# Input projection: query latent first, the other 1024 columns as seven Strassen products chained in four PSUM banks, and the local attention by halves of the rows

## The chip, the cores and the metric

One core of a Trainium2 chip. Five engines work side by side, each with an instruction queue of its own: TensorE (PE: matmuls and transposes into PSUM banks), VectorE (DVE), ScalarE (ACT), GpSimd (POOL) and SyncE (SP), which here only starts DMAs. They wait for each other by semaphores. The metric is the device time of one execution in microseconds (us); lower is better.

## The reference

One decoder block on 1024 rows of 1024 columns, all in fp32:

```python
h = rmsnorm(x, mix_norm_g)
proj = h @ w_in
# columns of proj: local q 512 | local k 128 | local v 128 | query latent 384 |
#                  key/value latent 256 | rope key 32 | two gates of 1024
qa, ka, va, q_lat, kv_lat, k_r, g_a, g_b = split(proj)
o_a = sliding_window_attention(rope(qa), rope(ka), va, sinks)      # 8 heads of 64, 2 k/v groups, window 128
cq, ckv = rmsnorm(q_lat), rmsnorm(kv_lat)
o_b = causal_attention(cq @ w_uq, ckv @ w_ukv, rope(k_r))          # 8 heads
y = sigmoid(g_a) * (o_a @ w_o_swa) + sigmoid(g_b) * (o_b @ w_o_mla)
x = x + y @ w_out
h = rmsnorm(x, ffn_norm_g)
x = x + (silu(h @ w_gate) * (h @ w_up)) @ w_down
return rmsnorm(x, final_norm_g)
```

The change touches the first matmul, `h @ w_in`, without the gates, and the local (sliding-window) attention behind it.

## The kernel before

**Exact products.** Every fp32 operand is split in a high and a low half (`split`, L259): ScalarE casts the high half (L260), VectorE takes the low half as a difference (L261). `mm3` (L263) makes each product of three matmuls, high by high, high by low, low by high. The first row block is done in raw fp32 instead (L604), before any half is there.

**Input projection, before.** The rows come as eight blocks of 128. For each block x is loaded twice: as it is (`load_xs`), to take the sum of squares (`square`, ScalarE, L498), and transposed (`load_xt`), as the operand. GpSimd turns the mean into an rsqrt (`rstd_of`, L397 and L400) and scales an identity by it (`dg`, L501); TensorE spreads that over all partitions (`rb`, L505); VectorE multiplies the transposed block by it (`normalize`, L508). Blocks 0 to 4 start unnormalised, and the factor is put in behind the product. The columns come in four groups: `kvq` (512: the second half of q, k, v), `qa` (256: the first half of q), `ql` (416: query latent and rope key) and `kl` (256: key/value latent), each for eight row blocks, each with eight steps of k by three matmuls. Behind them VectorE does the rotations (`rope_of`, L473 to L480) and GpSimd and VectorE the norms of the latents (`latent_end`, L780; `kv_out`, L1127). `h` is stored (`h_out`) and loaded again (`load_set`) to form t1 to t4 (`set_of_h`), the differences of quarters of h which the gates' Strassen products need.

**Gates.** They are done by class `Seven`: each pair of column blocks takes seven products of quarter size instead of eight. `mix` makes the sums of weights on GpSimd, `prep` splits them, `gate_step` runs one product. The first of them writes `fa`.

**Local attention.** Sixteen iterations, two k/v groups by eight row blocks, run between the gate products: per iteration three `gate_step`s, the transposed query (`sw_qT`, whose low halves `qs` VectorE makes at L1044 and L1045), the scores (`sw_scores`), exp, transposed probabilities, and the product with v.

**Order.** In this part of the program each engine's instructions stand in the order in which the code is written (`manual_schedule`, `by_hand`): the order was set by hand, a call after the other. Later stages have theirs from a planner, `Plan`, which takes steps with costs and ranks and writes out an order per engine.

Of the kernel before, what the change touches and what calls it, by code (L numbers as in the profile page):

```python
# [189 lines left out]
def hybrid_block_kernel(  # L190
# [129 lines left out]
    def split_g(hi, lo, raw, k0):  # L320
        for k in range(raw.shape[1]):
            g = gT[:, k0 + k:k0 + k + 1]
            nc.scalar.activation(hi[:, k], raw[:, k], AF.Copy, scale=g)
            nc.vector.scalar_tensor_tensor(lo[:, k], raw[:, k], g, hi[:, k].bitcast(F32), op0=ALU.mult,
                                           op1=ALU.subtract)

    def plain(key, src, shape, wide=False, k0=None):
# [95 lines left out]
    xs = {}  # L423
    xt = {}
    rb = {}

    def load_xt(b, pieces=1):
        xt[b] = U("xt", F32, (P, NK, P))
        n = NK // pieces
        for q in range(pieces):  # L430
            nc.sync.dma_start(xt[b][:, n * q:n * q + n], x_t[b][:, n * q:n * q + n])
            if b == 0 and q == 0:
                st.load_to(1)

    def load_xs(b):
        xs[b] = load_x(b)
# [1973 lines left out]
```

## Time and profile before

| | us |
|---|---|
| median of three runs | 1318.87 (1318.67, 1318.87, 1322.04) |
| span of the profiled execution | 1315.7 |
| its TensorE busy | 1305.2 |
| its VectorE, ScalarE, GpSimd busy | 931.0, 637.7, 568.3 |
| its first gate product starts | 138.25 |

The profiled execution has no time of its own beside its span: the span goes from the first to the last instruction, and the median of the runs lies 3.2 us above it, which is the work around the program. The profile's rows give for a group of instructions the line, the engine, the operation, the tiles with their shapes, the count, the busy time and the mean duration of one in nanoseconds, and then the idle time before them and what ended it. A timeline row gives start and length in us.

### The profile page before, as it was taken

Reading aid. Unit: us, or ns where it says so; the run is one execution under the profiler, and the core shown is the slowest. Engines: PE = TensorE matmul, PEld = TensorE weight load, DVE = VectorE, ACT = ScalarE, POOL = GpSimd, SP = SyncE. Lnnn points to the kernel's source line nnn. Section 1 sums busy time; section 2 is a strip of 40 time slices with the busy share of each in tenths; the row PEclk is TensorE's granted clock in tenths of the full one; section 3 lists DMA queues with packets and bytes.
Section 4 is the critical chain, followed back from the end, with each engine's and each line's share of the span. In section 5 each row is a group of like instructions: output and inputs, shape, how many; then the busy total and the mean of one; then the engine's idle time right before and its main releaser. Section 6 shows DMA issues by size and latency. Waiting matters only on the chain.

```text
span 1315.7 us, 18711 instructions
## 1 busy us (share of the span) xinstructions
PE 1305.2 (99%) x6463; PEld 1101.5 (84%) x6463; DVE 931.0 (71%) x1523; ACT 637.7 (48%) x1286; POOL 568.3 (43%) x552
## 2 busy tenths in 40 slices
PE   9999999999999999999999999999999999999997
PEld 6899888888888888888888888888888888888886
DVE  7868777766788874589889765776666555663964
ACT  7434667565578786644464232232323323634441
POOL 2126656553423266310234478775566621022521
PEclk9999999999999999999999999999999999999999
DMA  9454332336500112895231345753454335995504
GB/s 374 164 187 154 114 115 85 127 111 212 164 14 13 46 60 92 319 264 173 108 101 49 128 148 212 268 183 136 165 184 168 130 123 199 386 385 201 176 13 148
DMA packets 81534, 210.49 MB, mean 160 GB/s; under 512 B 9440, under 2 KB 16608, under 8 KB 80736
## 3 DMA queue, kind: packets, MB, share of 16 engines
q1 hardware_dynamic: 78560, 202.48, 43.6%
q0 software_dynamic: 1440, 4.72, 1.9%
q10 hardware_dynamic: 1440, 2.10, 0.5%
q8 instruction: 51, 0.84, 0.3%
q14 instruction: 43, 0.35, 0.1%
HBM read 143.34 MB, written 61.73 MB: 156 GB/s over the span
## 4 chain that ended last, share of the span: by engine, by line
PE 96%; DVE 1%; ACT 1%; DMA 1%; issue 1%; POOL 0%; SPq 0%; ACTq 0%; DVEq 0%; POOLq 0%
PE fa L269 8%; PE fa L268 8%; PE fa L267 8%; PE fb L269 6%; PE fb L268 6%; PE fb L267 6%; PE fd L268 5%; PE fd L269 5%; PE fd L267 5%; PE pTb L1581 2%; PE xo L269 2%; PE xo L268 2%; PE xo L267 2%; PE ob L1619 1%; PE scb L1536 1%; PE ob L1618 1%
## 5 line engine op out<-in xcount | busy, mean ns | idle before, releaser
L261 DVE TENSOR_TENSOR wl<-wr,wl 128x512 fp32r<-128x512 f32 x147 | 145.7, 1013 | 65.2 <-ACT wl L260 64.8
L261 DVE TENSOR_TENSOR lrv<-lr,lrv 128x1024 fp32r<-128x1024 f32 x77 | 104.9, 1395 | 49.8 <-ACT lrv L260 47.1
L260 ACT CAST lrv<-lr 128x1024 fp32r<-128x1024 f32 x77 | 80.1, 1052 | 95.8 <-PE fd L269 59.8
L268 PE MATMUL fd<-lrv 128*128 128x512 f32 x308 | 119.9, 389 | 0.4 <-DVE lrv L261 0.4
L267 PE MATMUL fd<-lrv 128*128 128x512 f32 x308 | 119.8, 389 | 0.0
L269 PE MATMUL fd<-lrv 128*128 128x512 f32 x308 | 119.8, 389 | 0.0
L260 ACT CAST wl<-wr 128x512 fp32r<-128x512 f32 x147 | 85.2, 621 | 3.6 <-DVE wr L962 1.8
L1565 POOL TENSOR_SCALAR p<-p,denb 128x384 f32<-128x384 f32 (+3 forms) x64 | 47.8, 748 | 89.3 <-DVE denb L1561 78.0
L261 DVE TENSOR_TENSOR wl<-sm,wl 128x512 fp32r<-128x512 f32 x59 | 54.3, 945 | 35.7 <-ACT wl L260 35.5
L275 POOL TENSOR_TENSOR wr<-wr,sm 128x512 f32<-128x512 f32 x20 | 30.1, 1506 | 94.2 <-DVE wl L261 94.2
L268 PEld LDWEIGHTS fd<-lrv 128*128 128x128 f32 x308 | 57.8, 188 | 12.9 <-DVE lrv L261 0.9
L267 PEld LDWEIGHTS fd<-lrv 128*128 128x128 f32 x308 | 57.8, 188 | 12.0
L269 PEld LDWEIGHTS fd<-lrv 128*128 128x128 f32 x308 | 57.8, 188 | 11.9
L397 POOL TENSOR_SCALAR ms<-ss 128x1 f32<-128x1 f32 x32 | 10.3, 323 | 113.1 <-ACT xn L2132 62.9
L2044 ACT ACTIVATE act<-sm 128x512 f32<-128x512 f32 x11 | 7.0, 633 | 104.1 <-DVE sm L272 104.1
L272 DVE TENSOR_TENSOR ptl<-pTb,pth 128x512 fp32r<-128x512 f32 (+2 forms) x96 | 49.5, 548 | 9.2 <-ACT pth L1592 8.8
L275 POOL TENSOR_TENSOR sm<-wr,wr 128x512 f32<-128x512 f32 (+1 forms) x36 | 42.0, 1174 | 31.7 <-PE fb L269 26.0
L1556 ACT ACTIVATE p<-scb,nmb 128x384 f32<-128x384 f32 (+3 forms) x64 | 47.9, 748 | 12.5 <-DVE nmb L1551 8.1
L1551 DVE CUSTOM_DVE_ANT_0 scb<-scb,mask 128x384 f32<-128x384 f32 (+3 forms) x64 | 48.3, 760 | 7.7 <-PE scb L1538 7.1
L1592 ACT CAST pth<-pTb 128x512 fp32r<-128x512 f32 (+2 forms) x96 | 43.1, 484 | 10.3 <-PE pTb L1581 10.0
L267 PE MATMUL fb<-t3h,wl 128*128 128x512 f32 x120 | 47.3, 394 | 0.0
L267 PE MATMUL fb<-t2h,wl 128*128 128x512 f32 x120 | 47.1, 393 | 0.0
(404 smaller groups left out, 4259.8 us busy)
## 6 DMA issues: line engine op xcount, KB each, us to landing
lr<-la_d SPq DMA_DIRECT2D x77, 256.0 KB, 5.4
wr<-in_w_gate_dram SPq DMA_DIRECT2D x22, 512.0 KB, 4.3
wr<-in_w_up_dram SPq DMA_DIRECT2D x22, 512.0 KB, 5.0
la_d<-sd SPq DMA_DIRECT2D x22, 512.0 KB, 5.0
wd<-in_w_down_dram SPq DMA_DIRECT2D x22, 512.0 KB, 7.0
rb_d<-wd SPq DMA_DIRECT2D x22, 512.0 KB, 2.6
lr<-rb_d SPq DMA_DIRECT2D x44, 256.0 KB, 5.4
lr<-in_w_down_dram SPq DMA_DIRECT2D x33, 256.0 KB, 5.4
```

The lines of the kernel that those rows point to most:

```text
L260: nc.scalar.copy(hi, src)
L261: (eng or nc.vector).tensor_tensor(lo, src, hi.bitcast(F32), op=ALU.subtract)
L267: nc.tensor.matmul(ps, ah, bh, start=first and i == 0, stop=False, skip_group_check=go_on)
L268: nc.tensor.matmul(ps, ah, bl, start=False, stop=False, skip_group_check=go_on)
L269: nc.tensor.matmul(ps, al, bh, start=False, stop=last and i == n - 1, skip_group_check=go_on)
L272: eng.tensor_tensor(out, a, b, op=ALU.subtract)
L275: eng.tensor_tensor(out, a, b, op=ALU.add)
L1551: nc.vector.tensor_tensor_reduce(s_, s_, m_, 1.0, -NEG, op0=ALU.add, op1=ALU.min, accum_out=nm)
L1556: nc.scalar.activation(p_, s_, AF.Exp, scale=-1.0, bias=t_.pop(("nm", key)), accum_out=den)
L1565: nc.gpsimd.tensor_scalar(p[:, 0:w], p[:, 0:w], den, 0.0, op0=ALU.mult, op1=ALU.add)
L1581: nc.tensor.transpose(pp[:, k], t_["p", key][:, blk(4 * g + k)], ident)
L1592: nc.scalar.copy(hi, pp)
```

## The change

**Query latent first.** TensorE's first row block, in raw fp32, is now one of `ql`'s; then `ql` for the row blocks in the order 0, 4, 1, 5, 2, 6, 3, 7 (`ROWS`). Blocks 0 and 4 are raw, that is, unnormalised; the others wait for `normalize`. The `square`s, `rb`s and so on are steps of a plan now.

**Seven products for the other 1024 columns.** The columns q, k, v and key/value latent are laid out as a matrix of two column blocks `f` by two halves `kh` of the 1024 k, and each quarter in two pieces `kp` (`load_left`: tiles `ws`). With rows 0 to 3 and rows 4 to 7 as the two row blocks, the product is done in Strassen's way. Scaled by the gain on ScalarE (`scale_left`, L1097), the pieces are summed on VectorE (`left_sum`: s0, s1, d1, d2) and split (tiles `wl`, 128x1024); t1 to t4 are formed at once from the normalised blocks, on GpSimd (`t_step`), and split. Product q, piece kp, for the rows t of a half is `product(q, kp, t)`, six matmuls of 512 columns, called (q,kp,t) here. Their order is q = 1, 2, 6, 7, 4, 5, 3, each with kp = 0, 1 and t = 0 to 3; 6 adds to the PSUM banks of 1, 7 to those of 6, 4 to those of 7, and 3 to those of 5. Tile `st` is the bank. ScalarE copies an intermediate state of a bank where it is an output (E1, W1, W2), VectorE adds to it what lies in the other banks (c11, C22, C12). Then come the rotations, and the norms of the key/value latent (`kv_square`, `rstd_in` on GpSimd as tile `rs_k`, `kv_norm` on VectorE, called k4).

**Order.** All engines' order in this stage comes out of a `Plan` named `beg`: `go(name, eng, cost, emit, after, ...)` adds a step, `rank_by_need` ranks each by when its users need it, and tiles are given out from numbered slots, so that a step can wait for the last reader of a slot.

**Stores.** h is no longer stored and loaded again.

**Local attention.** Its iterations are in the order group 0 rows 0 to 3, group 1 rows 0 to 3, group 0 rows 4 to 7, group 1 rows 4 to 7 (`ITS`). The work of rows 4 to 7 that was done in the projection is done between the iterations: v's halves and k's rotation (`late_row`), k's transposes (`late_k`), q's rotation (`late_q`). The sums over v come in four pieces (`V_AT`).

The core of the diff, with the new steps:

```diff
+    for i, b in enumerate(ROWS):
...
+            ps = tl_["ql", b] = (PX if i < 6 else P1)("ql", (P, 416))
+            mm3(ps, [(hT(k, blk(b)), (tl_["wq", k // 2][0][:, k % 2], tl_["wq", k // 2][1][:, k % 2])) for k in range(NK)])
...
+    def product(q, kp, t):
+        if kp == 0:
+            tl_["ps", q, t] = tl_["ps", {6: 1, 7: 6, 4: 7, 3: 5}[q], t] if q in (6, 7, 4, 3) else (PX if q == 1 else P1)("st")
+        wh, wl_, _ = tl_["left", q, kp]
+        hi, lo = quad[{1: (0, 0), 2: (1, 0), 3: (1, 1)}[q]] if q in (1, 2, 3) else hq[B_OF[q]]
+        mm3(tl_["ps", q, t], [((hi[:, k, blk(t)], lo[:, k, blk(t)]), (wh[:, k % 2], wl_[:, k % 2])) for k in (2 * kp, 2 * kp + 1)],
+            first=kp == 0 and q not in (6, 7, 4, 3), last=kp == 1, go_on=q in (6, 7, 4, 3))
...
+        go("rq", t, eng="D", cost=1450, after=[("M", 4, 1, t)] + [("rq", 0)] * (t == 1), emit=rope_q, use=(("U", ("rp", t)), ("U", ("qq", t))), free=(("rp", t),))
...
+        go("k4", t + 4, eng="D", cost=450, port=True, after=[("k3", t + 4)], emit=lambda t=t: kv_norm(half_of("w2", t)[:, 256:512], t + 4))
...
+    go("gx", eng="P", cost=4000, port=True, after=[("gs", 0), ("gs", 1), ("l", "g", 1), ("h", "g", 1)], emit=lambda: gates.mix(0, nc.gpsimd), use=(("U", "gsum"),))
...
+    def late_q(it):
+        b = ITS[it][1]
+        qn = sw[it]["qn"]
+        rope_nat(halves(qn[:, 0:256], 32), 4, 32, tl_["rope_a"][:, 0, b], tl_["rope_a"][:, 1, b], [halves(qn[:, 0:256], 32)])
```

Three places in the order of the engines. First ScalarE, where the third normalised row block (block 2) gets its high half. Before, casts of a block (`hh<-xt`) stand among squares and copies:

```order
L498 ACTIVATE x_305,ss_459<-x_305 128x1024
L583 COPY qn_452<-qn_452 128x256
L530 CAST khd_155<-kT_436 128x128
L530 CAST khd_156<-kT_436 128x128
L498 ACTIVATE x_307,ss_470<-x_307 128x1024
L260 CAST hh_147<-xt_131 128x4x128
L260 CAST hh_151<-xt_131 128x4x128
L260 CAST hh_149<-xt_303 128x4x128
L260 CAST hh_153<-xt_303 128x4x128
```

After, two scalings of a left factor (L1097) stand ahead of the casts of block 2 (`xt_258`), behind the norms of the latents (L997):

```order
L1006 COPY kr_331<-ql_343 128x32
L1097 ACTIVATE ws_378<-ws_378,gT 128x512 x2
L843 CAST hh_120<-xt_258 128x4x128
L843 CAST hh_124<-xt_258 128x4x128
L843 CAST hh_122<-xt_273 128x4x128
L843 CAST hh_126<-xt_273 128x4x128
L843 CAST wl_435<-ws_378 128x1024
L1097 ACTIVATE ws_385<-ws_385,gT 128x512 x2
L1097 ACTIVATE ws_394<-ws_394,gT 128x512 x2
L843 CAST wl_474<-ws_385 128x1024
L843 CAST wl_480<-ws_394 128x1024
```

The first left factor is scaled ahead of block 2's cast. Second, VectorE at the end of the projection. Before, from the first query's low halves (`qs`) to the first gate products' left factors (L962 scales, L1127 normalises a key/value latent block, L261 takes the low half):

```order
L1044 TENSOR_TENSOR qs_1445<-qT_1442,qs_1445 64x2x128
L1045 TENSOR_TENSOR qs_1445<-qT_1442,qs_1445 64x2x128
L962 TENSOR_SCALAR wr_1398<-wr_1398,gT 128x2x128 x4
L261 TENSOR_TENSOR wl_1522<-wr_1398,wl_1522 128x512
L1127 SCALAR_TENSOR_TENSOR lat_1429<-lat_1429,rstd_1435,lg_991 128x256
L962 TENSOR_SCALAR wr_1400<-wr_1400,gT 128x2x128 x4
L275 TENSOR_TENSOR sm_1564<-wr_1398,wr_1400 128x512
L272 TENSOR_TENSOR sm_1564<-sm_1564,wr_1398 128x512
L272 TENSOR_TENSOR wr_1398<-wr_1398 128x512
L1127 SCALAR_TENSOR_TENSOR lat_1477<-lat_1477,rstd_1483,lg_991 128x256
```

After, the last stretch ahead of product 3's second left low half (`wl_1244`): key/value norms (L1190), a gate's low half (`wl_1214`), the rotations of query blocks 2 and 3 (L454 to L457), `qs`:

```order
L295 TENSOR_TENSOR wl_1214<-sm_1177,wl_1214 128x512
L454 TENSOR_TENSOR rp_1218<-st_642,tab_650 128x256 x2
L456 TENSOR_TENSOR qn_1217<-rp_1218 128x4x32
L457 TENSOR_TENSOR qn_1217<-rp_1218 128x4x32
L454 TENSOR_TENSOR rp_1224<-st_668,tab_650 128x256 x2
L456 TENSOR_TENSOR qn_1223<-rp_1224 128x4x32
L457 TENSOR_TENSOR qn_1223<-rp_1224 128x4x32
L1190 SCALAR_TENSOR_TENSOR lat_1073<-st_642,rs_k,tab_278 128x256
L1190 SCALAR_TENSOR_TENSOR lat_1090<-st_668,rs_k,tab_278 128x256
L745 TENSOR_TENSOR qs_1237<-qT_1234,qs_1237 64x2x128
L746 TENSOR_TENSOR qs_1237<-qT_1234,qs_1237 64x2x128
L295 TENSOR_TENSOR wl_1244<-ws_431,wl_1243 128x1024
```

The rotations and norms, which were spread over the stage, stand in one row ahead of that left factor; on GpSimd the rsqrts for the norms (`rs_k`) stand around the sums of the gate's weights (`sm`, `wr`: `mix`). GpSimd before, at the same place:

```order
L397 TENSOR_SCALAR ms_1433<-ss_1431 128x1
L400 TENSOR_TENSOR rstd_1435<-ms_1433,neg_half 128x1
L397 TENSOR_SCALAR ms_1481<-ss_1479 128x1
L400 TENSOR_TENSOR rstd_1483<-ms_1481,neg_half 128x1
L397 TENSOR_SCALAR ms_1514<-ss_1512 128x1
L400 TENSOR_TENSOR rstd_1516<-ms_1514,neg_half 128x1
L397 TENSOR_SCALAR ms_1556<-ss_1554 128x1
L400 TENSOR_TENSOR rstd_1558<-ms_1556,neg_half 128x1
L397 TENSOR_SCALAR ms_1599<-ss_1597 128x1
L400 TENSOR_TENSOR rstd_1601<-ms_1599,neg_half 128x1
```

and after:

```order
L501 TENSOR_TENSOR rs_q<-rs_q,neg_half 128x1
L295 TENSOR_TENSOR xt_163<-xt_163,xt_174 128x256 x2
L501 TENSOR_TENSOR rs_q<-rs_q,neg_half 128x1
L501 TENSOR_TENSOR rs_k<-rs_k,neg_half 128x1 x5
L298 TENSOR_TENSOR sm_1177<-wr_993,wr_1033 128x512
L295 TENSOR_TENSOR sm_1177<-sm_1177,wr_993 128x512
L295 TENSOR_TENSOR wr_993<-wr_993 128x512
L501 TENSOR_TENSOR rs_k<-rs_k,neg_half 128x1
L295 TENSOR_TENSOR wr_1033<-wr_1033,sm_1177 128x256 x2
L501 TENSOR_TENSOR rs_k<-rs_k,neg_half 128x1 x2
```

The rsqrts of the last key/value blocks have moved behind the sums. Third, TensorE at the end of the stage. Before, the last key/value latent block (`kl`) stands just ahead of the first gate product:

```order
L267 MATMUL kl_1719<-wh_1144,hh_151 128x256
L268 MATMUL kl_1719<-wl_1145,hh_151 128x256
L269 MATMUL kl_1719<-wh_1144,hl_152 128x256
L267 MATMUL kl_1719<-wh_1144,hh_151 128x256
L268 MATMUL kl_1719<-wl_1145,hh_151 128x256
L269 MATMUL kl_1719<-wh_1144,hl_152 128x256
L267 MATMUL fa_1764<-hh_147,wl_1522 128x512
L268 MATMUL fa_1764<-hl_148,wl_1522 128x512
L269 MATMUL fa_1764<-hh_147,wl_1522 128x512
```

After, product 3 does, shown where its second piece begins:

```order
L290 MATMUL st_1106<-wl_1124,hh_126 128x512
L291 MATMUL st_1106<-wl_1125,hh_126 128x512
L292 MATMUL st_1106<-wl_1124,hl_127 128x512
L290 MATMUL st_1106<-wl_1124,hh_126 128x512
L291 MATMUL st_1106<-wl_1125,hh_126 128x512
L292 MATMUL st_1106<-wl_1124,hl_127 128x512
L740 MATMUL qT_1234<-ident,qn_1162 128x128 x2
L290 MATMUL st_1046<-wl_1243,hh_126 128x512
L291 MATMUL st_1046<-wl_1244,hh_126 128x512
L292 MATMUL st_1046<-wl_1243,hl_127 128x512
L290 MATMUL st_1046<-wl_1243,hh_126 128x512
```

The transposed query (`qT`) and product 3's second piece (`wl_1243`, `wl_1244`) follow the last product on its first piece (`wl_1124`); the gate product `fa` comes some 40 matmuls later.

More of the change, by code (lines that the diff above doesn't have):

```diff
@@ L318, in halves_of, with plain @@
         return U("wh", F32R, shape), U("wl", F32R, shape)
[L320 to L327, printed above, removed]
+    def plain(key, src, shape, wide=False):
         def load():
@@ L422, in hybrid_block_kernel @@
     in_order.__enter__()
[L423 to L436, printed above, removed]
+    xs, xt, rb = {}, {}, {}
     dgt = U("dg", F32, (P, 8, P))
@@ L789, in hybrid_block_kernel @@
+    make_identity(nc, ident)
+    for _ in range(11):
+        nc.tensor.matmul(P1("warm"), warm[:, 0:P], warm, start=True, stop=True)
+    del warm
+    tri = U("tri", F32, (P, P))
+    make_lower_triangular(nc, tri)
+    nc.vector.tensor_copy(below, tri)
+    del tri
     B_OF = {1: "b11", 2: "b21", 3: "b22", 4: "t4", 5: "t1", 6: "t2", 7: "t3"}
@@ L948, in hybrid_block_kernel @@
     sw = {}
+    ITS = [(g, b) for b0 in (0, 4) for g in range(NG) for b in range(b0, b0 + 4)]
     oa_t = {}
@@ new lines, in hybrid_block_kernel, with square, spread_row @@
+    for j in range(4):
+        go("wh", j, eng="A", cost=1240, emit=lambda j=j: ql_high(j), after=[("L", "w", j)], use=(("V", ("wq", j)),))
+        go("wl", j, eng="D", cost=1250, emit=lambda j=j: ql_low(j), after=[("wh", j)], port=True)
+        go("wf", j, eng="J", cost=0, after=[("wl", j), ("ql", 0)], emit=lambda j=j: tl_.pop(("wr", j)), free=(("wr", j),))
+    def square(b):
+        t = xs.pop(b)
+        nc.scalar.activation(t, t, AF.Square, accum_out=rn[:, b:b + 1])
+    def spread_row(b):
+        rb[b] = P1("rb", (P, P))
+        nc.tensor.matmul(rb[b], ones, dg[:, b % 7], start=True, stop=True)
@@ new lines, in hybrid_block_kernel, with ql_first, ql_row @@
+    go("df", eng="J", cost=0, after=[("sp", b) for b in ROWS], free=("dg",))
+    def ql_first(j):
+        if j == 0:
+            tl_["ql", 0] = PX("ql", (P, 416))
+        for k in (2 * j, 2 * j + 1):
+            nc.tensor.matmul(tl_["ql", 0], tl_["h0"][:, k], tl_["wr", j][:, k % 2], start=k == 0, stop=k == NK - 1)
+        if j == 3:
+            tl_.pop("h0")
+    def ql_row(i, b):
+        if b == 0:
+            ql_first(3)
+        else:
+            ps = tl_["ql", b] = (PX if i < 6 else P1)("ql", (P, 416))
+            mm3(ps, [(hT(k, blk(b)), (tl_["wq", k // 2][0][:, k % 2], tl_["wq", k // 2][1][:, k % 2])) for k in range(NK)])
+        if i == NB - 1:
+            for j in range(4):
+                tl_.pop(("wq", j))
@@ new lines, in gate_part, with gate_src @@
+    def gate_part(q, i):
+        key = (0, q, "g")
+        if key not in gates.left:
+            gates.left[key] = U("wl", F32R, (P, 2, 4, P))
+        return gates.left[key][:, i]
+    def gate_src(q):
+        return gates.sums[(0, "g")][:, 1] if q == 6 else gates.part(0, "g", *{1: (0, 0), 2: (1, 0)}[q])
+    for kh in range(2):
+        go("gs", kh, eng="A", cost=2050, after=[("L", "g", 0, kh)], emit=lambda kh=kh: gates.scale_part(0, kh))
+    go("gx", eng="P", cost=4000, port=True, after=[("gs", 0), ("gs", 1), ("l", "g", 1), ("h", "g", 1)], emit=lambda: gates.mix(0, nc.gpsimd), use=(("U", "gsum"),))
```

871 lines of the change are left out of this document (467 added, 404 removed).

## The prediction

> **What bounds the kernel now.** I read the page first: busy shares, clock, the chain that ended last.
>
> ```profile
> span 1315.7 us, 18711 instructions
> PE 1305.2 (99%) x6463; PEld 1101.5 (84%) x6463; DVE 931.0 (71%) x1523; ACT 637.7 (48%) x1286; POOL 568.3 (43%) x552
> PEclk9999999999999999999999999999999999999999
> PE 96%; DVE 1%; ACT 1%; DMA 1%; issue 1%; POOL 0%; SPq 0%; ACTq 0%; DVEq 0%; POOLq 0%
> ```
>
> TensorE is busy 99% of the span, at full clock, and is 96% of the chain. So a matmul that is removed is worth its own pitch, but only while the other engines keep ahead; and any new wait of TensorE adds its whole length. The timeline of TensorE gives the pitches (start to start) and the borders of the stage:
>
> ```profile
> 1.30 4.65 PE L592 MATMUL warm<-warm 128*128 128x512 bf16 x11 [1.30 <-DVE warm L589]
> 5.79 7.03 PE L604 MATMUL kvq<-wr,h 128*128 128x512 f32 x16
> 12.25 1.03 PE L552 MATMUL kvq<-wv,hh 128*128 128x512 f32 x2
> 16.33 1.98 PE L558 MATMUL kvq<-wv,hh 128*128 128x512 f32 x8
> 18.14 1.98 PE L552 MATMUL kvq<-wv,hh 128*128 128x512 f32 x8
> 35.48 0.28 PE L267 MATMUL qa<-wv,hh 128*128 128x256 f32 x1
> 35.59 0.28 PE L268 MATMUL qa<-wv,hh 128*128 128x256 f32 x1
> 77.60 0.35 PE L267 MATMUL ql<-wh,hh 128*128 128x416 f32 x1
> 77.79 0.35 PE L268 MATMUL ql<-wl,hh 128*128 128x416 f32 x1
> 138.25 0.40 PE L267 MATMUL fa<-hh,wl 128*128 128x512 f32 x1
> ```
>
> A product of 512 columns takes 0.227 us (eight in 16.33 to 18.14), of 256 columns 0.12, of 416 columns 0.19 (0.189 over a row of 24). The first row's raw fp32 products end at 12.25, and the first gate product `fa` starts at 138.25: all of the input projection lies between. The table of busy times by stretch shows the room beside it:
>
> ```profile
> 20.00:40.00 20.00, 20.00 (x111) 17.28 (x110) 18.08 (x39) 13.18 (x33) 6.25 (x12) 1.00 0.70 279
> 100.00:120.00 20.00, 20.00 (x126) 19.87 (x125) 17.74 (x40) 7.78 (x19) 13.35 (x19) 1.00 0.62 202
> 160.00:200.00 40.00, 40.00 (x201) 33.40 (x200) 29.44 (x59) 26.82 (x80) 25.51 (x32) 1.00 0.36 118
> ```
>
> Columns are TensorE, weight load, VectorE, ScalarE, GpSimd. TensorE has no gap in any of them, yet VectorE is 90% busy: it has about 2 us in 20 to spare.
>
> **The change: TensorE's work.** Before, 12.25 to 138.25 holds 168 products `kvq` of 512 columns, 384 of 256 (`qa`, `kl`) and 192 of 416 (`ql`). After, it holds 7 rows of `ql` (7x24x0.189 = 31.8 us), 336 Strassen products of 512 (x0.227 = 76.3) and 26 transposes and scores of 128 columns (at most the 256-column pitch, 3.1). From the same 12.25 that ends at 12.25 + 111.2 = 123.4, which is 14.8 before 138.25, if nothing waits. The raw row has 416 columns instead of 512 and could end 6.46x96/512 = 1.2 us sooner; row 4 then waits for the low halves of its weights on VectorE, so I count nothing. Of the 14.8, four pairs of `k` transposes (8x0.12 = 1.0) come back inside the local attention: they only moved.
>
> **Wait A, after row 4.** The `rb` (the row norms, spread) of rows 1 and 5 now stand behind row 4's 24 products. Behind them VectorE normalises row 1, then row 5, then ScalarE casts and VectorE takes the low half, before row 1 can run. The groups of instructions by shape, from the first 140 us (count, busy, mean ns):
>
> ```profile
> L508 DVE TENSOR_TENSOR xt<-xt,rb 128x1024 f32<-128x1024 f32 x8 | 9.7, 1215 | 0.1
> L261 DVE TENSOR_TENSOR hl<-xt,hh 128x512 fp32r<-128x512 f32 x24 | 15.5, 686 | 3.6 <-ACT hh L260 3.6
> L260 ACT CAST hh<-xt 128x512 fp32r<-128x512 f32 x24 | 13.6, 616 | 8.7 <-DVE xt L508 7.4 <-DMA xt<-in_x_t_dram 1.2
> L323 ACT ACTIVATE wv<-wr,gT 128x512 fp32r<-128x512 f32 x8 | 5.3, 714 | 1.3 <-DMA wr<-in_w_x_dram 1.3
> ```
>
> 1.215 + 0.616 + 0.686 = 2.5, with the `rb` 2.6. The bounds: 1.8 if the products start on the cast alone, 3.7 if row 5's normalising is in front of the low half for all its length (1.215 more).
>
> **Wait B, after row 5.** ScalarE's queue has `scale_left` of the first left factor (two of the 714 ns rows) ahead of the cast that row 2 needs, and that factor's load comes after eight blocks of x, eight of x transposed, the query-latent weights and a table: 16x0.524 + 1.70 + 0.46 + 0.52 = 11.1 MB.
>
> ```profile
> GB/s 0 35 247 365 393 358 363 332 410 418 418 426 403 402 395 430 406 406 401 426 406 406 401 426 406 406 401 399 395 418 414 410 410 246 37 0 8 0 0 0
> DMA packets 4035, 12.62 MB, mean 316 GB/s; under 512 B 576, under 2 KB 832, under 8 KB 4032
> ```
>
> This is the DMA view of the first 40 us, in slices of 1 us: 12.62 MB are in by 34, at some 410 GB/s, so 11.1 MB are in by 30.0, 30.5 with the last packets. Then 1.43 of scaling, 0.62 cast, 0.69 low: row 2 runs at 33.2. TensorE is free at 12.25 + 2.6 + 3x4.54 + 0.8 (`rb`) = 29.3. The wait is 3.8 (2.2 if the loads land a microsecond earlier and the low half is not awaited; 4.5 if later).
>
> **In the middle** VectorE and GpSimd share the stretch as they do not before: the sums for t1 to t4 go to GpSimd in pieces, while VectorE takes low halves. What that costs is in the timelines (VectorE three rows, GpSimd one):
>
> ```profile
> 93.84 0.68 DVE L261 TENSOR_TENSOR t1l<-hr,t1h 128x512 fp32r<-128x512 f32 x1
> 94.45 1.23 DVE L261 TENSOR_TENSOR t3l<-ht,t3h 128x512 fp32r<-128x512 f32 x1
> 95.60 1.23 DVE L261 TENSOR_TENSOR t2l<-ht,t2h 128x512 fp32r<-128x512 f32 x1
> 94.01 2.27 POOL L272 TENSOR_TENSOR h<-hr,ht 128x256 f32<-128x256 f32 x2 [0.81 <-DVE ht L272]
> ```
>
> The same low half takes 0.68 alone and 1.23 beside GpSimd's subtraction. 16 low halves of t by 0.55 are 8.8 us more of VectorE at worst, over some 70 us in which it has about 7 to spare. On SP's queue the last two loads of left factors now stand behind seven stores of latent rows, each of which waits for its row, so the sums for product 6 begin late. I take 2.0 of wait for both, where the low halves of product 6 are late; ends 0 and 6.
>
> **The tail, at product 3.** Only three products and a transpose (18x0.227 + 0.25 = 4.3 us) lie between product (5,1,3) and (3,1,0), whose left low half VectorE makes. In VectorE's order stand ahead of it: the query ropes of rows 0 to 3, a sum, seven key/value normalisations (`k4`), a gate low half and the first `qs`. The rope of row 0 needs a buffer that product (5,1,3) is the last to read; GpSimd's gate sums (`mix`) need that rope's buffer in turn, and stand ahead of the rsqrt of key/value rows 5, 6 and 7, for which `k4` waits. The groups and single rows of the same kinds:
>
> ```profile
> L473 DVE TENSOR_TENSOR rp<-qa,ra 128x256 f32<-128x256 f32 x16 | 6.0, 416 | 0.0
> L479 DVE TENSOR_TENSOR qn<-rp 128x128 f32<-128x128 f32 x8 | 2.3, 292 | 0.3
> L480 DVE TENSOR_TENSOR qn<-rp 128x128 f32<-128x128 f32 x8 | 2.3, 285 | 0.0
> 139.02 0.47 DVE L1127 SCALAR_TENSOR_TENSOR lat<-lat,rstd,lg 128x256 f32<-128x256 f32 x1
> 142.82 0.42 DVE L1044 TENSOR_TENSOR qs<-qT,qs 64x256 fp32r<-64x256 f32 x1
> 143.27 0.43 DVE L1045 TENSOR_TENSOR qs<-qT,qs 64x256 fp32r<-64x256 f32 x1
> L275 POOL TENSOR_TENSOR sm<-wr,wr 128x512 f32<-128x512 f32 (+1 forms) x36 | 42.0, 1174 | 31.7 <-PE fb L269 26.0
> L400 POOL TENSOR_TENSOR rstd<-ms,neg_half 128x1 f32<-128x1 f32 x15 | 9.6, 642 | 1.3
> L272 POOL TENSOR_TENSOR ht<-ht 128x256 f32<-128x256 f32 x8 | 5.8, 748 | 10.9 <-DMA hr<-h_d 5.8 <-DVE hr L272 5.1
> L261 DVE TENSOR_TENSOR lrv<-lr,lrv 128x1024 fp32r<-128x1024 f32 x77 | 104.9, 1395 | 49.8 <-ACT lrv L260 47.1
> ```
>
> By the sum so far (5,1,3) ends at 12.25 + 31.8 + 294x0.227 + 1.0 (`rb`) + 2.6 + 3.8 + 2.0 = 120.1. In a row of instructions on VectorE each starts about 0.08 before the last one's record ends (93.84, 94.45: 0.61 for 0.68). A rope is then 2x0.34 + 0.21 + 0.21 = 1.1. GpSimd, from 121.2: three sums of 512 (1.17 each, 1.5 beside VectorE), three rsqrts (0.64), two pieces (0.75 each): 7.0 to 8.5, the last rsqrt at 128.2 to 129.7, say 129.2. VectorE from there: two `k4` (0.8), the gate low half 0.6, two ropes 2.2, two `k4` 0.8, two `qs` 0.85, and the low half of a left factor of 128x1024 (1.15 alone by twice a half row; 1.4 in the last row): 6.4. It is done at 135.6; TensorE is there at 124.4. The wait is 11.2; I take 10.8, since its first `k4` can lie ahead. Bounds: 6.0 if the rsqrts are in time (VectorE alone, from 120.1: four ropes 4.4, sum 0.6, seven `k4` 2.8, 0.6, 0.85, 1.15 = 10.4, less 4.3), 13 if each instruction of the two meets the other. So `fa` starts at 123.4 + 2.6 + 3.8 + 2.0 + 10.8 = 142.6, against 138.25: 4.4 later.
>
> **The local attention** runs beside the gate products; by the row of 160 to 200 above VectorE is 74% busy there, GpSimd 64%, TensorE 100%. Eight query ropes (1.1), and `k` rope and low halves of four rows, come to VectorE there: some 14 us over twelve iterations of 10.8, that is 1.2 on top of 8 each. That fits; it costs 0 to 3, and I take nothing. At its start a sum of a gate product now stands ahead of the two `qs` low halves of the second iteration, and the scores behind them wait:
>
> ```profile
> 144.94 0.69 DVE L275 TENSOR_TENSOR pu<-fb,pu 128x512 f32<-128x512 f32 x1
> ```
>
> Its input is a product that TensorE finishes just before those scores; 0.6 + 0.85 and the handing over are 1.5 (0 to 3). The dropped store and reload of h free DMA time only: TensorE had no gap there.
>
> The total: 4.4 + 1.0 + 1.5 = 6.9 on the median 1318.9 (the profiled span is 1315.7, so 3.2 lie outside it in the median, and stay): 1325.8, said as 1326.
>
> **Rivals.** (1) *The tail is half covered.* If the buffers of the first rope and of the gate sums are free before, the rsqrts are in time and the tail is its lower end, 6.0 in place of 10.8: 1321.0. With less wait in the middle, 1319: no difference. For it: GpSimd is idle a third of 100 to 120 before (13.35 of 20 busy). Against: its order now has the sums of t there. (2) *Faster.* The one mechanism: product 3's left low half is not late, because VectorE reaches it before (5,1,3) ends; the tail is 0, and `fa` starts at 131.8: 1318.9 - 6.4 + 2.5 = 1315.0, and 1311 to 1313 if A or the middle is at its lower end too. It decides at a tail of under 6: each microsecond of VectorE's queue that lies earlier is a microsecond less. Against it stand 18.08 and 17.74 of 20 us already busy. (3) *TensorE slows after its idle times.* The 11 warm-up products took 4.65 us, 0.42 each, against 0.227 later: if 10.8 us without work bring TensorE back to that, and it lasts as long as the warm-ups, it costs 4.65x(1 - 0.227/0.42) = 2.1 after the tail, and as much after B: 1328 to 1330. Before has no gap like it, so no row shows whether it does. The Trainium skill, TensorE: Matmul & The Clock Gate, Part 1: The HAM clock gate, speaks for it: an idle window of about 3.4 us halves the clock, and 3.4 us of work restore it. By its figure (an estimate) one fall costs 3.4/2 = 1.7 us, both 3.4, and the time would be 1327.5 to 1329. (4) *VectorE and GpSimd hold each other up* all through the middle, 6 us: 1330.
>
> **How the numbers follow.** A measurement of this kernel tells about 0.3%, 4 us, from no change; so faster is under 1314.9, slower over 1322.8. My forecast as it stands has 0.34, at 1326; with the clock of rival 3, 0.16; rival 4, 0.10: slower 0.60. Rival 1, 0.23. Rival 2, 0.17. The range goes from 1313, the middle of rival 2, to 1335, where rivals 3 and 4 come together with late loads (1326 + 4 + 4 + 1); outside of it lie some 0.09 below and 0.07 above. The likeliest case's own range is 1322 to 1331.
>
> **What the profile after would show.** TensorE's first row ends near 12; then idle of 2 to 3 us put down to VectorE's low half of row 1, near 17, and of some 4 before row 2, near 29, put down to ScalarE's cast. The products of 512 run 0.227 apart. The longest idle time of all stands before product (3,1,0), near 124 to 135, put down to VectorE; in VectorE's rows just before it, a wait on GpSimd's rsqrt, and in GpSimd's, three gate sums ahead of it. `fa` starts at 142 to 144. Behind that, TensorE keeps 99% busy and the iterations of the local attention 10.8 us. The clock row shows whether a slice near 5 and 11 is below 9. The prediction is wrong if `fa` starts before 138 (the tail is not there), or if the local attention's iterations are over 11 us (VectorE bounds them).

## The result, and the profile after

The change made the kernel slower: 1341.03 us, the median of four runs (1340.34 to 1342.97), against 1318.84 in the same comparison (1318.67 to 1322.04). The ratio is 1.0167, with an interval of 1.0153 to 1.0181. The forecast was 1326.0 with a range up to 1335: the direction was right, the size three times too small (22.2 us and not 7).

The page of the changed kernel, with the lines that answer to those shown before:

```profile
span 1341.3 us, 18193 instructions
PE 1303.8 (97%) x6223; PEld 1088.5 (81%) x6223; DVE 950.8 (71%) x1529; ACT 650.6 (49%) x1299; POOL 585.6 (44%) x553
PEclk9999899999999999999999999999999999999999
PE 84%; DVE 4%; DMA 4%; ACT 3%; issue 2%; POOL 2%; SPq 1%; DVEq 0%; POOLq 0%; ACTq 0%
```

TensorE has 240 instructions fewer, and yet only 1.4 us less of busy time; of its share of the chain it lost 12 points, and VectorE, ScalarE, GpSimd and the DMAs have them. The profiled execution lasted 1342.97 us, the longest of the four: what follows is its decomposition, 25.6 us of span. It is more than the 22.2 of the medians because the span of a run lies 1.7 us below its time (1341.3 for 1342.97): the profiled execution after lies 1.9 above its median, and the one before, with its span of 1315.7, some 1.4 below. The 3.2 us between that span and the median are thus only in part the work around the program.

TensorE's timeline up to the first gate product (start, length; in brackets the idle time before, and what ended it):

```profile
12.36 0.67 PE L290 MATMUL ql<-wv,hh 128*128 128x416 f32 x1
...
19.57 0.45 PE L290 MATMUL ql<-wv,hh 128*128 128x416 f32 x1 [1.74 <-ACT hh L843]
20.65 0.72 PE L292 MATMUL ql<-wv,hl 128*128 128x416 f32 x1 [0.44 <-DVE hl L295]
...
33.28 1.04 PE L950 MATMUL rb<-dg 128*128 128x128 f32 x4 [1.40 <-POOL dg L964]
...
136.53 0.80 PE L290 MATMUL st<-wl,hh 128*128 128x512 f32 x1 [8.64 <-ACT wl L843]
138.50 0.80 PE L291 MATMUL st<-wl,hh 128*128 128x512 f32 x1 [1.17 <-DVE wl L295]
139.09 0.63 PE L292 MATMUL st<-wl,hl 128*128 128x512 f32 x1
...
148.28 0.50 PE L290 MATMUL fa<-hh,wl 128*128 128x512 f32 x1 [0.32 <-DVE khd L295]
```

`fa` starts at 148.28, 10.0 us later than before. Below, an idle time is counted as what a start-to-start distance has above the usual one for that shape; this is a few tenths more than the bracket where the product behind the wait is slow too. So counted, the 136 us from 12.36 hold 111.1 of work, 20.9 of waits and 3.9 of products at half clock (0.63 long where they are 0.39 elsewhere, 0.43 apart and not 0.227).

From `fa` to the end of the local attention it takes 194.8 us, before 179.0: 15.8 more. Behind that, 998.2 and 998.5 us: no difference. TensorE's waits in the local attention (sum, times, longest):

```profile
PE fa L290 <- DVE es L775: 4.8, 1, 4.8
PE sc L759 <- DVE qs L745: 2.8, 2, 1.5
PE fa L290 <- DVE go L298: 1.3, 1, 1.3
PE sc L759 <- DVE qs L746: 0.6, 3, 0.2
```

Before, this stage had no row of TensorE's waits at all. The waits stand in three iterations: from one group of transposed probabilities to the next it takes 14.6, 17.8 and 12.3 us there, and 9.5 to 11.4 in the other twelve (before: 9.6 to 10.9 in all fifteen). With the idle ahead of smaller pieces, 11.4 of the 15.8 are waits; 3.6 are half clock, 0.6 the `k` transposes that moved here. The table of busy times by stretch shows the clock (TensorE's busy time first; the last three columns are granted clock, DMA share, GB/s). The stretches are set where the granted clock changes:

```profile
16.84:20.25 3.41, 1.63 (x9) 1.08 (x7) 2.61 (x3) 2.51 (x5) 0.21 (x1) 1.00 1.01 405
20.26:23.66 3.40, 3.01 (x9) 2.91 (x10) 2.99 (x7) 2.90 (x6) 2.98 (x3) 0.50 1.05 348
129.49:132.90 3.41, 0.00 (x0) 0.00 (x0) 2.26 (x7) 0.43 (x1) 2.51 (x4) 1.00 0.22 79
132.90:143.13 10.23, 5.43 (x12) 3.96 (x13) 6.38 (x16) 2.07 (x4) 0.00 (x0) 0.50 0.26 90
187.51:190.91 3.40, 1.80 (x12) 1.65 (x13) 2.44 (x6) 3.11 (x10) 1.59 (x3) 1.00 0.20 77
190.92:194.33 3.41, 3.41 (x9) 2.64 (x8) 3.37 (x16) 1.50 (x5) 3.41 (x6) 0.50 0.00 0
228.47:231.87 3.40, 1.17 (x8) 0.76 (x6) 0.83 (x2) 1.19 (x4) 1.99 (x3) 1.00 0.00 0
231.88:238.70 6.82, 4.27 (x10) 3.43 (x11) 6.44 (x19) 3.45 (x13) 1.49 (x2) 0.50 0.48 150
```

Four waits are each followed by half clock, for 3.4, 10.2, 3.4 and 6.8 us. In the second and the fourth of these, part of the time is the wait itself, in which a slow clock costs nothing. They cost 1.3, 2.3, 1.6 and 2.0 us, 7.1 of the 25.6. The page's clock row averages over slices of 34 us and shows one 8, no more.

**The longest wait of the local attention**, at 229.4, is led back by the rows of three engines. GpSimd:

```profile
227.07 1.42 POOL L295 TENSOR_TENSOR wr<-wr 128x256 f32<-128x256 f32 x2
228.46 1.28 POOL L295 TENSOR_TENSOR vt<-vv 128x512 f32<-128x512 f32 x1
229.81 0.72 POOL L298 TENSOR_TENSOR vt<-vt 128x256 f32<-128x256 f32 x1
```

and then ScalarE and TensorE:

```profile
222.13 0.62 ACT L283 CAST wl<-wr 128x512 fp32r<-128x512 f32 x1
230.57 0.40 ACT L283 CAST vd<-vt 128x256 fp32r<-128x256 f32 x1 [7.82 <-POOL vt L298]
...
234.43 0.76 PE L290 MATMUL fa<-hh,wl 128*128 128x512 f32 x1 [4.79 <-DVE es L775]
```

The third of the four pieces of the sums over v (`vt`, new with `V_AT`) stands on GpSimd behind a chain of gate sums (`sm`, `wr`) and the softmax sums (`den`), busy without a gap from 220.7. ScalarE's cast of it (`vd`) stands in front of the key casts and the next left factor, and holds the queue for 7.8 us. TensorE's row names VectorE (`es`). But VectorE had itself stood for 6.2 us until ScalarE's cast (its low half of `vd`, at 231.01), and then had 3.2 us of other work ahead of `es`. The releaser that a row names is only the last link.

**The tail, at product 3.** VectorE, with one row of ScalarE, and GpSimd of the changed kernel:

```profile
129.65 0.74 DVE L1190 SCALAR_TENSOR_TENSOR lat<-w,rs_k,tab 128x256 f32<-128x256 f32 x1
131.52 1.00 DVE L1190 SCALAR_TENSOR_TENSOR lat<-w,rs_k,tab 128x256 f32<-128x256 f32 x2 [1.12 <-POOL rs_k L501]
133.04 0.75 DVE L454 TENSOR_TENSOR rp<-st,tab 128x256 f32<-128x256 f32 x2
...
137.22 1.23 DVE L295 TENSOR_TENSOR wl<-ws,wl 128x1024 fp32r<-128x1024 f32 x1
...
134.67 0.36 ACT L743 CAST qs<-qT 64x256 fp32r<-64x256 f32 x1 [4.75 <-DVE qn L457]
```

```profile
124.98 1.29 POOL L298 TENSOR_TENSOR sm<-wr,wr 128x512 f32<-128x512 f32 x1 [2.69 <-issue]
126.35 1.29 POOL L295 TENSOR_TENSOR sm<-sm,wr 128x512 f32<-128x512 f32 x1
127.60 1.26 POOL L295 TENSOR_TENSOR wr<-wr 128x512 f32<-128x512 f32 x1
128.83 0.59 POOL L501 TENSOR_TENSOR rs_k<-rs_k,neg_half 128x1 f32<-128x1 f32 x1
129.39 1.58 POOL L295 TENSOR_TENSOR wr<-wr,sm 128x256 f32<-128x256 f32 x2
130.94 1.06 POOL L501 TENSOR_TENSOR rs_k<-rs_k,neg_half 128x1 f32<-128x1 f32 x2
```

Three gate sums stand ahead of the rsqrts (`rs_k`), VectorE waits 1.12 for the last of these, and the low half (137.22) comes behind the ropes: the place and the order that were forecast. TensorE's row puts the first 8.64 down to ScalarE, whose cast of the same left factor stands behind two `qs` casts; these had stood 4.75 for VectorE's rope, so that piece too leads back to VectorE. The wait itself is 8.80 + 1.73 + 0.37 = 10.9.

### The profile page after: what moved, and what is told of

Its sections match the earlier page's. It is cut to its first block, busy times and chain, and to the rows that moved or that the text cites. A ratio compares the mean times of both kernels' runs of the same rounds, so it can differ in the third digit from the quotient of the medians.

```text
span 1341.3 us, 18193 instructions
## 1 busy us (share of the span) xinstructions
PE 1303.8 (97%) x6223; PEld 1088.5 (81%) x6223; DVE 950.8 (71%) x1529; ACT 650.6 (49%) x1299; POOL 585.6 (44%) x553
## 4 chain that ended last, share of the span: by engine, by line
PE 84%; DVE 4%; DMA 4%; ACT 3%; issue 2%; POOL 2%; SPq 1%; DVEq 0%; POOLq 0%; ACTq 0%
PE fa L290 8%; PE fa L292 7%; PE fa L291 7%; PE fb L292 6%; PE fb L290 6%; PE fb L291 6%; PE fd L290 5%; PE fd L291 5%; PE fd L292 5%; PE pTb L1739 2%; PE xo L292 2%; PE xo L291 2%; PE xo L290 2%; PE ob L1777 1%; PE scb L1694 1%
## 5 line engine op out<-in xcount | busy, mean ns | idle before, releaser
L1723 POOL TENSOR_SCALAR p<-p,denb 128x384 f32<-128x384 f32 (+3 forms) x64 | 47.8, 749 | 89.6 <-DVE denb L1719 75.6
L1714 ACT ACTIVATE p<-scb,nmb 128x384 f32<-128x384 f32 (+3 forms) x64 | 47.8, 747 | 11.6 <-DVE nmb L1709 8.0
L2202 ACT ACTIVATE act<-pu 128x512 f32<-128x512 f32 x22 | 13.9, 633 | 67.8 <-DVE pu L295 36.2
```

Of the source, the lines that this page charges most:

```text
L1714: nc.scalar.activation(p_, s_, AF.Exp, scale=-1.0, bias=t_.pop(("nm", key)), accum_out=den)
L1723: nc.gpsimd.tensor_scalar(p[:, 0:w], p[:, 0:w], den, 0.0, op0=ALU.mult, op1=ALU.add)
```

## The experiments

**Which waits, and which releasers.** Theory A took the rows above as they stand; theory B, where the text names it, is a rival for the same place. Four edits, one at a time.

`e1` puts the casts of the v sums at the end of an iteration in the code:

```diff
-        if it - 1 in V_AT:
-            v_parts(*V_AT[it - 1])
         gate_step()
...
             sw_exp(it + 1)
+        if it - 1 in V_AT:
+            v_parts(*V_AT[it - 1])
```

> The halves of the summed v (`v_parts`, cast on ScalarE, low half on VectorE) stand at the end of the iteration, behind the exps, instead of in its middle. In the trace of the changed kernel ScalarE waits 7.8 us at 222.8 to 230.6 for GpSimd's sums of v with that cast at the head of its queue, TensorE then idles 4.8 us at 229.6 and runs at half clock until 238.4. Theory A (the place of the cast in ScalarE's queue makes that wait): 5.0 of idle time and 2.0 of half clock go, and up to 1.5 at 282.7: 1341.0 down to 1333 (1331 to 1336). Theory B (VectorE's and GpSimd's additional work bounds the iterations, the wait only shows at this cast): the idle time moves to the next iteration, 1341 +- 2.

1344.31 us (1341.78 to 1345.0), ratio 1.0196 (1.0182 to 1.021): no gain, but 3.3 more; where from was not traced. The edit did not reach what it meant to move. In the local attention the order of ScalarE, VectorE and GpSimd is the scheduler's; only TensorE's and SP's is written by hand (`by_hand` ends ahead of its loop, in both kernels). The cast of the third piece kept its place and the wait stayed, at 4.6. This run says nothing for or against the cause, which e5 settles.

`e2` puts the gate sums behind the last three rsqrts:

```diff
-    go("gx", ..., after=[("gs", 0), ("gs", 1), ("l", "g", 1), ("h", "g", 1)], ...
+    go("gx", ..., after=[("gs", 0), ("gs", 1), ("l", "g", 1), ("h", "g", 1), ("k3", 5), ("k3", 6), ("k3", 7)], ...
```

> The gate sums on GpSimd stand behind the rsqrts of key/value rows 5 to 7; the planner also puts product 3's second low half ahead of the rope of row 3 and of the query's low halves. Theory A (the prediction's tail: the rsqrts behind the gate sums and VectorE's queue hold TensorE before product (3,1,0)): the wait of 8.8 + 1.7 us there falls to 5 to 7, less 4 to 5 us, and the gate's low half comes later, which may cost up to 2 at the second gate product: 1336 to 1339. Theory B (VectorE's ropes and norms alone fill that time; the trace shows only 1.1 us in which VectorE waited for an rsqrt): 1340, and only as far as product 3's low half has moved up.

1336.33 us (1335.55 to 1338.54), ratio 1.0139 (1.0125 to 1.0152): 4.7 less than the change. Its waits of TensorE from 110 to 140:

```profile
PE st L291 <- DVE wl L295: 4.2, 1, 4.2
PE st L290 <- ACT wl L843: 2.7, 1, 2.7
```

In place of 10.9 the wait is 2.9 + 4.4 + 0.4 = 7.7. The gate sums' place is thus worth more than the 1.12 us that VectorE visibly waits for, but the run does not price it alone: with the new rule the plan puts `wl` ahead of the last rope too. What is left is VectorE's own queue.

`e3` lets TensorE do 60 more transposes, of no use, into the free half of `qT`'s bank, where the 8.8 us of idle are:

```diff
+        for _ in range(60 if it == 0 else 0):
+            nc.tensor.transpose(ptf[:, 2], qn[:, blk(0)], ident)
```

> 60 transposes more of the first query (some 8 us of TensorE) behind the two that are needed, into the unused half of their bank, in the 8.8 us in which TensorE waits for product 3's low half. They change no result and no other engine's work. Theory A (TensorE's clock falls after time without work and costs on its own): the granted clock stays 1.0 through 133 to 143, the 24 products behind take 0.227 instead of 0.43 at first, 1341.0 less 2.2: 1338.8 (1338 to 1339.5). Theory B (the slow products are slow for another reason, or the low halves pace them): 1341 +- 0.7. If the transposes delay the query's low halves, up to 1 us more.

1341.81 us (1340.99 to 1343.11), ratio 1.0178 (1.0164 to 1.0192): no gain. The idle went from 8.8 + 1.7 to 2.3 + 1.8, but from 138.3 on there is half clock again, which costs 1.4 us (2.3 before). `e6`, below, tries more.

`e4` lets the first scaling of a left factor wait for the casts of block 2, which the prediction had put behind it (wait B):

```diff
-    emit=lambda ...: scale_left(f, kh, kp), after=[("L", "l", f, kh, kp)])
+    emit=lambda ...: scale_left(f, kh, kp), after=[("L", "l", f, kh, kp), ("bh", 2, 1)])
```

> All scalings of left factors wait for the casts of row block 2, so that the cast stands ahead of the first scaling in ScalarE's queue. Theory A (the prediction's wait B: the scaling and its load hold row 2): row 2 starts 1.4 to 2 us sooner, 1339 to 1339.6, if it isn't lost before product 3. Theory B (by the trace TensorE waits there 1.4 us for the last scaled identity of GpSimd, which stands behind a subtraction for t; the cast follows anyway): 0 to 0.3 at that place, 1341 +- 0.7.

1342.06 us (1340.72 to 1342.88), ratio 1.0178 (1.0164 to 1.0192): no gain. ScalarE now casts ahead of the scaling, and TensorE waits as before for GpSimd, in this run from 28 to 36:

```profile
PE rb L950 <- POOL dg L964: 0.9, 1, 0.9
PE rb L950 <- POOL xt L295: 0.5, 1, 0.5
```

So ScalarE's order alone did not make wait B. In GpSimd's rows of the changed kernel two t subtractions (`xt<-xt`, 30.16, 1.42 long), two rsqrts and a short product stand ahead of the `dg` at 32.85. But ScalarE's rows of the same kernel do show the scalings ahead of the cast, as the prediction had it:

```profile
32.14 1.33 ACT L1097 ACTIVATE ws<-ws,gT 128x512 f32<-128x512 f32 x2 [0.17 <-DMA ws<-in_w_s_dram]
33.38 2.17 ACT L843 CAST hh<-xt 128x512 fp32r<-128x512 f32 x4
```

The first of these casts ends near 34.0, and TensorE goes from the last `rb` to the products at 34.07: two chains that end together, of which the row names one.

**The local attention.** `e5` computes the late pieces of the v sums on VectorE:

```diff
-        sub(t, vt[:, r0 + 1:r1 + 1, g]..., vt[:, r0:r1, g]..., nc.gpsimd)
-        add(t[:, :, 0:HD], t[:, :, 0:HD], t[:, :, HD:P], nc.gpsimd)
+        e = nc.vector if r0 else nc.gpsimd
+        sub(t, vt[:, r0 + 1:r1 + 1, g]..., vt[:, r0:r1, g]..., e)
+        add(t[:, :, 0:HD], t[:, :, 0:HD], t[:, :, HD:P], e)
```

> The two late pieces of the sums over v (rows 4 to 7, one for each group) are made on VectorE instead of GpSimd; the engines' order of casts stays with the scheduler. Theory A (ScalarE and with it TensorE wait at 222 to 234 because those sums stand at the end of GpSimd's queue, behind the gate's sums): the wait of 4.8 us and the half clock of 2.0 behind it go, and 1.4 at 282: 1341 down to 1334 (1332 to 1336). Theory B (VectorE is the bound of these iterations, so 1.1 us more on it makes it no better): 1340 to 1342, the idle time in the same iterations.

1334.92 us (1334.53 to 1335.27), ratio 1.0124 (1.011 to 1.0138): 6.1 less than the change. Its row of the same cast on ScalarE, and its waits of TensorE from 190 to 300:

```profile
225.26 0.41 ACT L283 CAST vd<-vt 128x256 fp32r<-128x256 f32 x1 [4.16 <-DVE vt L298]
```

```profile
PE sc L760 <- DVE qs L747: 0.3, 2, 0.2
PE fa L290 <- DVE es L776: 0.2, 1, 0.2
```

The wait of 4.96 is 0.36 now, the half clock behind it is gone (2.0), and so is the wait at 282.7 (1.5). ScalarE still stands 4.2 us, and TensorE does not feel it. So the place of those sums on GpSimd was the cause; that it acts through ScalarE's held queue is read from the rows, and no run changed that queue alone. The wait at 187 stays (1.25 + 0.48, after 1.63 + 0.48 in the changed kernel) and was not traced further.

`e6` is e3 with 80 transposes.

```diff
+        for _ in range(80 if it == 0 else 0):
```

> 80 instead of 60 transposes more behind the first query's, so that TensorE has work through nearly all of the 8.8 us; with 60 there were still 2.3 + 1.8 us without work and the clock fell to half for 1.4 us of lost time. Theory A (the clock follows TensorE's time without work): no slice under 1.0 between 130 and 145 in the clock's row, 2.2 us less than the changed kernel in the profile up to the first gate product, 1338.8 in the median. Theory B (the clock falls whatever TensorE does there): 1341, half clock again at 138.

1342.51 us (1341.13 to 1343.43), ratio 1.0181 (1.0167 to 1.0195). Its table by stretch, behind the filled gap:

```profile
138.31:141.71 3.40, 1.77 (x7) 1.24 (x8) 1.85 (x3) 0.82 (x1) 0.00 (x0) 1.00 0.03 10
141.72:145.13 3.41, 3.41 (x11) 2.62 (x10) 1.65 (x3) 0.54 (x3) 0.00 (x0) 0.50 0.11 38
```

With 2.1 and 1.0 us of idle left, the clock still falls, at 141.7, 2.5 us after the first product behind the gap (139.18), and costs 1.3 us. Filling a gap without closing it saved at most a microsecond of half clock in the traces, and nothing that the times show.

`e7` is the kernel before, with the order of iterations by halves (`ITS`) and the four pieces of the v sums (`V_AT`), and nothing else of the change.

```diff
+    ITS = [(g, b) for b0 in (0, 4) for g in range(NG) for b in range(b0, b0 + 4)]
+    V_AT = {0: (0, 0, 3), 2: (1, 0, 3), 6: (0, 3, 7), 10: (1, 3, 7)}
-        if it in (0, 5):
-            v_sums(it // 5)
+        if it in V_AT:
+            v_sums(*V_AT[it])
```

> The kernel before, with one part of the change alone: the local attention in the order of the halves and the sums over v in four pieces. All rows' k, v and q are ready before it. Theory A (the late work of rows 4 to 7, which the change moved in between, makes the waits there): 1318.8 +- 2, no wait over 1 us in the local attention. Theory B (the four pieces on GpSimd, in the middle of the gate's sums, make the wait, whenever the rows are ready): the wait of some 5 us at the third piece and half clock behind it, 1324 to 1327.

1322.90 us (1321.48 to 1326.01) against 1318.20, ratio 1.0029 (1.0016 to 1.0041): 4.7 slower. Its profiled run, the longest of six, waits 1.6 us at 154.4 and 2.3 at 219.6, with a half clock of 1.6 behind each. From `fa` to the end of the local attention that run takes 7.7 us more than before. The pieces and the order thus cost something without the late work of rows 4 to 7, about half of the 15.8 at most. Neither theory had that.

`e8` leaves the late rotations of q (`late_q`) out of the computation.

```diff
-        if it + 2 < N_SW and ITS[it + 2][1] > 3:
-            late_q(it + 2)
```

> The changed kernel without the rotations of the queries of rows 4 to 7 in the local attention (left out of the computation). Theory A (their 8 x 1.1 us on VectorE are covered): 1341 +- 1.5. Theory B (they make VectorE late, at 282 and in part at 229): 1.5 to 5 us less, 1336 to 1339.5.

1340.36 us (1337.42 to 1341.69), ratio 1.0162 (1.0148 to 1.0177). The added rotations of q are not the cause of the long wait: the one at 282.7 goes, the long one (4.3 here) stays.

**Together, and the rest.** `e9` is e2 and e5 in one.

> The two edits that helped, together: GpSimd's gate sums behind the rsqrts of key/value rows 5 to 7 (alone 4.7 us less), and the late sums over v on VectorE (alone 6.1 us less). Theory A (two separate waits of TensorE, one at product 3, one in the local attention): they add, 1341.0 - 4.7 - 6.1 = 1330 (1329 to 1332). Theory B (one of them shifts the other): 1333 to 1336.

1330.85 us (1328.4 to 1331.44), ratio 1.0079 (1.0065 to 1.0093). The two gains add (4.7 + 6.1 from 1341.03 is 1330.2).

`e10` is e9, with the rotations of query rows 2 and 3 moved from the tail into the local attention. ScalarE copies the rows out of PSUM instead:

```diff
+            else:
+                qns["q", t] = U("qn")
+                nc.scalar.copy(qns["q", t][:, 0:256], c_of(4)[:, 0:256])
...
-        if it + 2 < N_SW and ITS[it + 2][1] > 3:
+        if it + 2 < N_SW and (ITS[it + 2][1] > 3 or it < 2):
```

> As the run with both edits, and the rotations of the queries of rows 2 and 3 taken out of VectorE's queue ahead of product 3: ScalarE copies them out of the bank, and VectorE rotates them in the local attention like those of rows 4 to 7. The planner then sets product 3's second low half some ten instructions earlier, ahead of all key/value norms of rows 4 to 7. Theory A (the tail is VectorE's queue ahead of that low half, and nothing else): the waits at product 3, 7 us in the run with the rsqrts first, fall to under 2, and so does the half clock behind them: 1330 - 5 to 8 = 1322 to 1326. Theory B (what stood in the queue is late elsewhere: the first scores and the first gate products wait for it): 1327 to 1331.

1323.09 us (1321.96 to 1324.82) against 1319.51, ratio 1.0029 (1.0017 to 1.004): 7.8 less than e9. The wait at product 3 is gone, and `fa` starts at 137.28, 1.0 ahead of before. The tail was VectorE's queue. What its TensorE waits for up to 138, the longest three, and from 137 to 330, the longest two:

```profile
PE st L291 <- DVE wl L295: 2.4, 2, 1.3
PE rb L951 <- POOL dg L965: 2.3, 1, 2.3
PE ql L290 <- ACT hh L844: 1.7, 1, 1.7
...
PE sc L760 <- DVE qs L746: 1.9, 2, 1.7
PE sc L760 <- DVE qs L747: 0.7, 4, 0.2
```

Its local attention takes 187.1 us, 8.2 more than before: it gives back more than the projection gains. And the projection gains only 1.0 of the 14.8 us of saved products: the first row ends 1.0 later than before, and the waits A, B and of the middle, with the clock's fall behind B (1.3), are still there.

`e11` is e10 with the first t subtractions behind the `dg` of block 7, against wait B:

```diff
-    need = {1: [("nm", c), ("nm", z), ("bl", c, 0)], ...
+    need = {1: [("nm", c), ("nm", z), ("bl", c, 0), ("dg", 7)], ...
```

> As the run before in this list, and GpSimd's subtractions for t only behind the last scaled identity (dg of row 7). Theory A (the prediction's wait B is GpSimd's queue: rb of the last row waits for its dg behind a subtraction): the waits of 1.2 to 2.6 us near 31 to 34 go, 1.5 to 2 us less than the run before. Theory B (the t's are then late for product 6 and 7, and the middle takes it back): 0 to 2 us more, with waits near 70 to 95.

1329.53 us (1329.06 to 1329.64), ratio 1.0075 (1.0063 to 1.0088): 6.4 slower than e10, theory B. Wait B is gone. (ScalarE's casts of block 2 also stand ahead of the scalings in this run, at 29.33 and 32.67, so it does not tell GpSimd's share from ScalarE's.) Its waits of TensorE from 28 to 140 are now

```profile
PE st L290 <- DVE lat L1016: 4.7, 1, 4.7
PE st L291 <- DVE wl L295: 3.8, 2, 3.0
```

The subtractions that were late at 30 are late at 69 and 79, where they are dearer, and two falls of the clock come with them (2.0, 1.4); a third (1.5) follows three waits of 1.0 to 1.3 between 120 and 126 that e10 does not have.

`e12` is e10 with the iterations in the order of before (group 0, then group 1), the late rows in the first five and the pieces of the v sums moved to fit (only the first line of the edit is shown).

```diff
-ITS = [(g, b) for b0 in (0, 4) for g in range(NG) for b in range(b0, b0 + 4)]
+ITS = [(g, b) for g in range(NG) for b in range(NB)]
```

> As the run with the rotations of rows 2 and 3 moved (1323.1), but the local attention in the order of before, group 0 rows 0 to 7 and then group 1; the late work of rows 4 to 7 stands in the first five iterations, one row in each, and the sums over v of group 1 behind it. Theory A (what is left against before, some 8 us in the local attention, is the order by halves, as the run of before with the halves alone gave 4.7 us): 1318 to 1320, the waits near 143 and 179 gone. Theory B (it is the late work of rows 4 to 7 on VectorE and ScalarE, which is now crowded into fewer iterations): 1323 to 1328, with waits in the first five iterations.

1324.09 us (1322.48 to 1324.7), ratio 1.0036 (1.0023 to 1.005): as e10, and its local attention takes 186.8. With these repairs, the order by halves is not what is left. Its waits of TensorE there are again for `qs`, 2.0 us in two, and for `go`, 1.4 (theory B). No version beat the kernel before.

## Why the prediction was wrong, step by step

- **TensorE's work: right.** 111.2 was forecast, 111.1 measured from the first row's end (12.36 for 12.25). The products saved are really saved.
- **Wait A: right** in place and size: 2.6 forecast, 1.91 + 0.60 measured. The row was to name VectorE's low half; ScalarE's cast ended the 1.91, and the low half only the 0.60.
- **Wait B: size too large, half of the cause missed.** 3.8 forecast, 1.56 + 0.26 + 0.34 = 2.2 measured. The step put it on ScalarE's `scale_left`, which does stand there; but e4 took that away and the time did not move, because GpSimd's `dg` for the last `rb` was as late. e11, with both out of the way, has no wait there. I had read ScalarE's queue and the loads, not the `rb`'s own input.
- **The middle:** 2.0 forecast, 0.76 + 1.36 + 1.30 = 3.4 measured, inside its ends; the 6 of rival 4 did not come.
- **The tail: right.** 10.8 forecast, 10.9 measured, before the very product and behind the very rows, all about 3 us later than the sum had it (TensorE there at 127.6 and not 124.4). GpSimd's terms add up to 6.9 to 7.9 and not to the 7.0 to 8.5 of the step; from 124.98 to 132.0 it took 7.0. e2 and e10 took it away by the two causes that the step named: the gate sums ahead of the rsqrts, and the ropes ahead of the low half. Rivals 1 and 2, with a shorter tail, were wrong.
- **Waits before `fa` in all:** 19.2 forecast, 20.9 measured; the rest of 1.9 is handing over between products.
- **The clock: the mechanism of rival 3 came true,** which had a chance of 0.16; its time, 1328 to 1330, did not. The forecast as it stood had no fall. The rival had two, 2.1 each, after the tail and B. There were four in the profiled run, after the tail (2.3), A (1.3) and two waits of the local attention (1.6, 2.0), and none after B. The Trainium skill, TensorE: Matmul & The Clock Gate, Part 1: The HAM clock gate, says an idle window of about 3.4 us halves the clock. After the tail the trace agrees (3.41 us without work from 129.49 on, half clock from 132.90); after A and at 187 it does not, since 2.5 and 2.1 us of idle were enough.
- **The local attention: the step that failed.** "It costs 0 to 3, and I take nothing" stood beside 1.5 at its start. The start was right (1.45 + 0.43). The rest measured 9.5 of waits and 3.6 of half clock. The step summed VectorE's load, which indeed fits: twelve of fifteen iterations keep their length, and e8, with some 8.8 us less of it, is 0.7 faster. It never asked where the four pieces of the v sums stand on GpSimd, or what on ScalarE waits for them; e5 moved the two late pieces and gained 6.1. The prediction's own sign, iterations over 11 us, came (11.6 in the mean), but by three single waits and not because VectorE bounds them. The order of VectorE, ScalarE and GpSimd in this stage is the scheduler's, before and after, so a call moved in the code can land anywhere in an engine's queue.

The sum: of the 18.7 us that the profiled run lies above the forecast's steps (25.6 for 6.9), 9.5 are waits in the local attention, 7.5 half clock (all pieces), 1.7 waits before `fa`.

Why the change is 22 us slower is then shown by runs for the most part: the tail (e2, e10) and the v sums (e5) give back 18 with the clock falls behind them. Why even so nothing is left of the 14.8 us of saved products is read from e10's trace, not shown by a run: 13.8 of them are lost ahead of `fa`, in the late first row, the waits A, B and of the middle, one fall of the clock and the handing over, and 8.2 us more in the local attention. e11 ended B and lost more elsewhere. How much the late work costs by itself stays open: e8 left out only q's rotations, on top of the unrepaired waits.

## What to carry to other kernels

When TensorE is 99% busy, a change that removes products and moves the work between them is priced by queues and not by loads: for every moved step, look at what stands ahead of it on its engine and who stands behind the one that waits for it, in the later stages too. A wait that leaves TensorE idle for more than about half of 3.4 us should be booked with 1.3 to 2.3 us more for the clock, unless the trace excludes it. A rule that puts one step behind another is cheap to try and can as well make it worse: e2 won 4.7 us by one, e11 lost 6.4.
